# Feed-forward activations in six tiles of their own, at six addresses mod 1024, where one address served all moving tiles

## The chip, the cores and the metric

The kernel runs on one core of a Trainium2 chip. The metric is the device time of one launch in microseconds. Lower is better.

## What is computed

Two layers of a decoder trunk over 256 tokens with 1024 features. Each layer has a feed-forward, four token mixers in parallel, a second feed-forward, and an input embedding under a gate:

```python
def swiglu(u, w_gu, w_down):
    gate, up = jnp.split(u @ w_gu, 2, axis=-1)
    return (jax.nn.silu(gate) * up) @ w_down

for i in range(DEPTH):                                   # DEPTH = 2, D_FF = 2816
    h = h + 0.5 * swiglu(rms_norm(h, ffn1_norm[i]), ffn1_w_gu[i], ffn1_w_down[i])
    h = h + token_mixing(rms_norm(h, mix_norm[i]), ...)  # DeltaNet, mLSTM, S5, MoBA, gates, w_out
    h = h + 0.5 * swiglu(rms_norm(h, ffn2_norm[i]), ffn2_w_gu[i], ffn2_w_down[i])
    h = h + (p[i] @ ple_w_proj[i]) * jax.nn.sigmoid(rms_norm(h, ple_norm[i]) @ ple_w_gate[i])
return rms_norm(h, final_norm)
```

## The kernel before

Features lie on the partitions and the 256 tokens along the free dimension. Every float32 product is made of three matmuls on rounded halves (`mm3`): weights are split into `wh` and `wl`, activations into a high and a low tile, and wh·high, wh·low and wl·high are added in PSUM. Each of the three loads its 128x128 stationary weights anew and streams 256 columns of 4 bytes, so a moving operand is 1024 bytes per partition. In the mixers' transposed projections (`mm3t`) the roles are swapped: there a slice of the activations `xa` is stationary, and the weights `wh`, `wl` move.

Weights arrive by DMA in units of 128x1024 (`raw`). ScalarE rounds a unit to `wh`, and VectorE subtracts to get `wl`. There are four `raw` buffers and six each of `wh` and `wl`.

A feed-forward (`ffn`) runs over 22 tiles f of 128 hidden features. For each f, the gate and up products are 48 matmuls with the moving tiles `xa0`, `xa1` (or, in the second feed-forward of a layer, a tile of the same kind). VectorE and ScalarE then make the activation `act2`: its high half by a copy on ScalarE, its low half by a subtraction on VectorE. With a lag of two tiles (`LAG = 2`), the down product of f - 2 follows: eight output tiles by three matmuls, 24 matmuls with the moving tile `act2`, into four PSUM banks named `acc` (three) and `inv` (one). Down products of the last two tiles come at the end, bank by bank.

`act2` is a tile of the tag `A`, one of four buffers. Tags `A`, `B`, `Y` and `D` lie in the pool `operands` together with `xa0` and `xa1`, behind a pad of `BASE` = 288 bytes. All their sizes are multiples of 1024 bytes, so all of these tiles start at the same address mod 1024, which the title of the change gives as 416. Behind that pool comes the pool of constants, and then the pool of weights behind a pad of `WBASE` bytes; a slice of weights is 512 bytes wide.

The order of the instructions is not the order of the source. A planner (`Plan.order`) runs a list schedule over all instructions with a cost for each, and issues them in the order that it finds. A tile of a tag takes one of the tag's buffers in that schedule, and waits if none is free. The planner's cost of a matmul is the longer of its columns and twice its weights' columns at 2400 per us, and then

```python
(0.007 if views[2].store.tag.startswith("xa") else 0.011)
```

All instructions are issued from one line, 430, which is why tiles and not lines tell them apart in the profile.

## Time and profile before

| what | value |
|---|---|
| time, median of 3 runs | 1336.62 us (1332.21, 1336.62, 1351.59) |
| time of the profiled execution | 1337.75 us |
| its span, from first to last instruction | 1336.0 us |
| TensorE busy share | 98% |
| VectorE, ScalarE busy share | 75%, 55% |
| matmuls | 11366, each with a weight load of its own |

The page's first part gives the busy time of each engine. The second gives the span in 40 slices, with the granted TensorE clock in tenths. Matmuls overlap in the pipeline, so the duration of one matmul (some 0.28 us) is longer than the distance from its start to the start of the next. That distance, here called the pitch, is what the time is made of. It can be read from a table of stretches: the matmuls counted in a stretch are those that overlap it, so the pitch is the width of the stretch plus one duration of 0.28 us, divided by the count.

### The profile page before, as it was taken

How to read it: one execution, taken by the hardware profiler on the slowest of the kernel's cores; microseconds unless marked ns; L12 is line 12 of the kernel's file. 1: busy time of each engine (PE TensorE's matmuls, PEld its weight loads, DVE VectorE, ACT ScalarE, POOL GpSimd, SP SyncE). 2: the span in 40 equal slices, each digit the busy share in tenths (PEclk: the TensorE clock that was granted, in tenths of full speed). 3: DMA queues.
4: the chain of work that ended last, by engine and by line, in shares of the span. 5: the costliest groups of instructions: out<-in, count | busy, mean ns of one | idle time of the engine just before them, and what ended most of it. 6: DMA issues, size and time to landing. Idle time of an engine off the chain costs nothing.

```text
span 1336.0 us, 27989 instructions
## 1 busy us (share of the span) xinstructions
PE 1315.3 (98%) x11366; PEld 1293.7 (97%) x11366; DVE 1003.0 (75%) x1893; ACT 739.7 (55%) x1174; POOL 39.1 (3%) x73
## 2 busy tenths in 40 slices
PE   8999999999999999999999999999989999999997
PEld 7999999988999999999999999999989999999997
DVE  7999557988858866666999965778876778655575
ACT  7655457884445644444655454689635456444453
POOL 2000000000010000000020000000000100000000
PEclk9999999999999999999999999999989999999998
DMA  8665565436636655555566645553466356555651
GB/s 291 182 192 166 187 194 161 147 105 145 204 114 194 189 191 190 191 194 206 166 218 193 190 147 188 173 182 103 136 149 214 110 176 201 197 194 194 203 167 54
DMA packets 81761, 233.67 MB, mean 175 GB/s; under 512 B 20832, under 2 KB 24928, under 8 KB 81632
## 3 DMA queue, kind: packets, MB, share of 16 engines
q1 hardware_dynamic: 81632, 231.88, 55.1%
q8 instruction: 89, 1.46, 0.4%
q14 instruction: 40, 0.33, 0.1%
HBM read 229.49 MB, written 2.36 MB: 174 GB/s over the span
## 4 chain that ended last, share of the span: by engine, by line
PE 88%; DVE 5%; issue 3%; DMA 2%; ACT 1%; SPq 1%; POOL 0%; DVEq 0%; POOLq 0%; ACTq 0%
PE mm L430 63%; PE acc L430 18%; PE inv L430 7%; DVE wl L430 2%; DMA raw<-dm 1%; ACT wh L430 1%; DVE C L430 1%; SPq L430 1%; DMA raw<-in_weights 1%; DVE s5u L430 1%; DMA xc<-in_x 0%; DMA q<-dx 0%; DVE B L430 0%; DVE T L430 0%; DVE A L430 0%
## 5 line engine op out<-in xcount | busy, mean ns | idle before, releaser
L430 PE MATMUL mm<-xa,wh 128*128 128x256 f32 x4288 | 757.6, 279 | 0.7 <-ACT wh L430 0.7
L430 ACT CAST wh<-raw 128x1024 fp32r<-128x1024 f32 (+1 forms) x434 | 437.1, 1038 | 457.4 <-issue 212.9
L430 PEld LDWEIGHTS mm<-xa,wh 128*128 128x128 f32 x4288 | 654.5, 189 | 4.0 <-ACT wh L430 1.2
L430 PE MATMUL mm<-xa,wl 128*128 128x256 f32 x2144 | 598.4, 279 | 0.6 <-DVE wl L430 0.6
L430 DVE TENSOR_TENSOR wl<-raw,wh 128x1024 fp32r<-128x1024 f32 (+1 forms) x434 | 514.1, 1207 | 48.3 <-ACT wh L430 47.5
L430 PEld LDWEIGHTS mm<-xa,wl 128*128 128x128 f32 x2144 | 404.1, 188 | 2.3 <-DVE wl L430 1.3
L430 DVE TENSOR_TENSOR T<-mm,rs 128x512 f32<-128x512 f32 x98 | 67.4, 689 | 171.2 <-PE mm L430 169.6
L430 PE MATMUL acc<-A,wh 128*128 128x256 f32 x1056 | 187.2, 278 | 2.7 <-ACT A L430 2.7
L430 PEld LDWEIGHTS acc<-A,wh 128*128 128x128 f32 x1056 | 160.8, 189 | 3.0 <-ACT A L430 2.9
L430 PE MATMUL acc<-A,wl 128*128 128x256 f32 x528 | 146.2, 278 | 0.0
L430 PE MATMUL mm<-B,wh 128*128 128x256 f32 x576 | 101.0, 278 | 0.0
L430 PEld LDWEIGHTS acc<-A,wl 128*128 128x128 f32 x528 | 99.4, 188 | 0.0
L430 PEld LDWEIGHTS mm<-B,wh 128*128 128x128 f32 x576 | 87.3, 188 | 0.6 <-ACT B L430 0.4
L430 PE MATMUL mm<-B,wl 128*128 128x256 f32 x288 | 79.9, 279 | 0.0
L430 PE MATMUL inv<-A,wh 128*128 128x256 f32 x352 | 65.5, 278 | 0.0
L430 PEld LDWEIGHTS mm<-B,wl 128*128 128x128 f32 x288 | 53.9, 188 | 0.0
L430 PEld LDWEIGHTS inv<-A,wh 128*128 128x128 f32 x352 | 53.8, 189 | 0.0
L430 DVE TENSOR_TENSOR th<-mm,rs 128x512 f32<-128x512 f32 (+1 forms) x41 | 27.6, 676 | 31.4 <-PE mm L430 27.6
L430 PE MATMUL mm<-wh,xa 128*128 128x256 f32 (+1 forms) x256 | 49.3, 285 | 0.0
L430 PE MATMUL inv<-A,wl 128*128 128x256 f32 x176 | 48.8, 277 | 0.0
L430 ACT CAST A<-sg 128x256 fp32r<-128x256 f32 x88 | 35.3, 402 | 14.7 <-DVE sg L430 14.6
L430 PEld LDWEIGHTS mm<-wh,xa 128*128 128x128 f32 x256 | 40.1, 188 | 0.7
(263 smaller groups left out, 1352.8 us busy)
## 6 DMA issues: line engine op xcount, KB each, us to landing
raw<-in_weights SPq DMA_DIRECT2D x420, 512.0 KB, 4.3
raw<-in_weights SPq DMA_DIRECT2D x8, 256.0 KB, 5.1
raw<-in_weights SPq DMA_DIRECT2D x4, 408.0 KB, 3.6
dm<-D SPq DMA_DIRECT2D x4, 256.0 KB, 4.5
raw<-dm SPq DMA_DIRECT2D x16, 64.0 KB, 4.5
out_t<-T SPq DMA_DIRECT2D x4, 256.0 KB, 2.5
xc<-in_x SPq DMA_DIRECT2D x3, 256.0 KB, 4.7
raw<-in_weights SPq DMA_DIRECT2D x2, 272.0 KB, 3.0
```

The source lines that it names most:

```text
L430: getattr(getattr(nc, v.engine), v.name)(*map(real, v.args), **{k: real(x) for k, x in v.kw.items()})
```

## The change

The feed-forwards' `act2` leaves the tag `A`. A new pool `acts` between `operands` and the constants holds six tiles `act0` to `act5`, one buffer each, and hidden tile f takes number f mod 6. Each is 16 columns (64 bytes) longer than its two halves, so that tiles follow each other at steps of 64 bytes mod 1024; the pool begins with a pad of 192 bytes, and `ACTS` gives the columns by which the halves are shifted inside their tile. With 416 as the address of the pool `operands`, the starts are 416 + 192 = 608, then 672, 736 + 64 = 800, 800 + 64 = 864, 864 + 48 = 912 and 928 + 16 = 944 mod 1024. `WBASE` falls from 736 to 160, since the new pool adds 192 + 6 x 2112 = 12864 bytes, which is 576 mod 1024: the weights keep their address mod 1024. All other tiles of the tags `A`, `B`, `Y`, `D` and `xa0`, `xa1` keep theirs.

```diff
-BASE, WBASE = 288, 736
+BASE, WBASE = 288, 160
+ACTS = (0, 0, 16, 16, 12, 4)
...
         self.op.tile([128, BASE // 4], F, tag="pad", name="pad")
+        self.ap = E(tc.tile_pool(name="acts", bufs=1))
+        self.ap.tile([128, 48], F, tag="pad", name="pad")
         self.cp = E(tc.tile_pool(name="const", bufs=1))
...
-            act2 = self.t("A", [128, 2, T], R)
+            at = ACTS[f % len(ACTS)]
+            act2 = nc.tile(self.ap, [128, 2 * T + 16], R, f"act{f % len(ACTS)}", 1)
+            act2 = act2[:, at:at + 2 * T].rearrange("p (a t) -> p a t", a=2)
             ah, al = act2[:, 0], act2[:, 1]
```

## Rows read from the trace of the kernel before

**Rows 1.** The page: engines' busy time, and the granted clock in 40 slices.
```profile
PE 1315.3 (98%) x11366; PEld 1293.7 (97%) x11366; DVE 1003.0 (75%) x1893; ACT 739.7 (55%) x1174; POOL 39.1 (3%) x73
PEclk9999999999999999999999999999989999999998
```

**Rows 2.** Waits of TensorE, whole run: total us, times, longest us.
```profile
PE acc L430 <- DVE D L430: 6.3, 2, 3.5
PE acc L430 <- ACT A L430: 2.7, 1, 2.7
PE mm L430 <- ACT sq L430: 1.6, 1, 1.6
```

**Rows 3.** Groups by form, TensorE, whole run: count | busy us, mean ns | idle before.
```profile
L430 PE MATMUL acc<-A,wh 128*128 128x256 f32 x1056 | 187.2, 278 | 2.7 <-ACT A L430 2.7
L430 PE MATMUL acc<-A,wl 128*128 128x256 f32 x528 | 146.2, 278 | 0.0
...
L430 PE MATMUL inv<-A,wh 128*128 128x256 f32 x352 | 65.5, 278 | 0.0
L430 PE MATMUL inv<-A,wl 128*128 128x256 f32 x176 | 48.8, 277 | 0.0
```

**Rows 4.** Stretches of TensorE: us, busy (matmuls), granted clock, DMA share, GB/s.
```profile
34.00:114.00 80.00, 80.00 (x708) 1.00 0.63 192
127.50:203.50 76.00, 76.00 (x647) 1.00 0.59 187
216.20:220.80 4.60, 4.60 (x39) 1.00 0.80 241
248.50:253.50 5.00, 5.00 (x45) 1.00 0.59 178
324.00:374.00 50.00, 50.00 (x427) 1.00 0.59 186
...
466.30:634.00 167.70, 167.70 (x1482) 1.00 0.59 194
677.40:766.00 88.60, 88.60 (x784) 1.00 0.63 197
775.80:857.80 82.00, 82.00 (x698) 1.00 0.54 174
870.40:875.00 4.60, 4.60 (x38) 1.00 0.76 223
902.60:907.80 5.20, 5.20 (x46) 1.00 0.55 182
983.00:1030.00 47.00, 47.00 (x417) 1.00 0.62 191
...
1122.50:1290.00 167.50, 167.50 (x1480) 1.00 0.59 195
```

**Rows 5.** Two of those stretches again, matmuls with tile A alone.
```profile
127.50:203.50 76.00, 32.08 (x261) 1.00 0.59 187
775.80:857.80 82.00, 32.56 (x264) 1.00 0.54 174
```

**Rows 6.** Order of time, TensorE, 126 to 128 us: start, us, count.
```profile
126.20 0.39 PE L430 MATMUL mm<-xa,wh 128*128 128x256 f32 x2
126.43 1.04 PE L430 MATMUL mm<-cst,C 128*128 128x128 f32 x8
127.22 0.36 PE L430 MATMUL mm<-xa,wl 128*128 128x256 f32 x1
127.42 0.40 PE L430 MATMUL acc<-A,wh 128*128 128x256 f32 x2
```

**Rows 7.** Groups by form in 216.2 to 220.8 us, matmuls of the swapped kind.
```profile
L430 PE MATMUL mm<-wh,xa 128*128 128x272 f32 x26 | 5.0, 289 | 0.0
```

**Rows 8.** Order of time, TensorE, around 230 us: the narrowest frequent moving operand.
```profile
230.00 2.34 PE L430 MATMUL acc<-C,B 128*128 128x64 f32 x20
232.15 0.36 PE L430 MATMUL mm<-xa,wh 128*128 128x256 f32 x1
```

**Rows 9.** Instructions of tile A, 482 to 492 us: ns min/median/max, first start.
```profile
L430 ACT CAST A<-sg x1: 400/400/400, 486.7 to 486.7; 128x256 fp32r<-128x256 f32 x1
L430 DVE TENSOR_TENSOR A<-sg,A x1: 417/417/417, 488.0 to 488.0; 128x256 fp32r<-128x256 f32 x1
```

## The prediction

> **What bounds the kernel now.** I read the page first, then TensorE's waits, its groups by form, and a table of stretches. The page [rows 1] shows TensorE busy 98% of the span, at the full granted clock nearly throughout; VectorE and ScalarE have room. The waits [rows 2] show that TensorE hardly waits: its three longest groups are 6.3, 2.7 and 1.6 us of 1336. So the time is the number of matmuls times the pitch, the distance from one start to the next, and only the pitch, the count or a new wait can move it.

> The pitch is what the table of stretches is for [rows 4]. Take width plus 0.28 us over the count. The stretch 466.3 to 634 gives 167.98 / 1482 = 113.35 ns, and 34 to 114, 677 to 766, 983 to 1030 and 1122 to 1290 give 113.4, 113.4, 113.4 and 113.4. But 127.5 to 203.5 gives 76.28 / 647 = 117.9, 775.8 to 857.8 gives 82.28 / 698 = 117.9, and 324 to 374 gives 117.8. The granted clock is 1.00 in all of them, so this is not the clock. The program is the same kind in both: the first layer's first feed-forward runs its first half at 113.4 and its second half at 117.9, with the same tiles at the same addresses. So one and the same matmul has two steady pitches, 4.5 ns apart (the short and the long one below), and keeps the one that it has. Order of time shows what switches it [rows 6]: at 126.4 us eight small transposes come in between, and behind them the long pitch begins. Within a stretch the pitch outlives the changes from `xa` to `A` and back, since both kinds stand in the stretches counted above. Thus with `xa` and `A` at one address mod 1024 the pitch is something that is handed on.

> **The change part by part.**

> *Counts.* Matmuls with the moving tile `act2` are the groups on `acc` and `inv`: 1056 + 528 + 352 + 176 = 2112 [rows 3], which is 4 feed-forwards x 22 tiles x 24. None is added or removed. The other matmuls of the feed-forwards are 4 x 22 x 48 = 4224, so a feed-forward matmul is an `act2` one in a third of the cases. In the two long-pitched stretches lie 647 + 698 = 1345 feed-forward matmuls [rows 4], 261 + 264 = 525 of them on `A` [rows 5]. I count the other 2112 - 525 = 1587 on `A`, and 4224 - 820 = 3404 on `xa` or its like, as short-pitched.

> *The pool and its buffers.* The planner could change its order if an activation ever waited for a buffer. It does not: f is made while f - 1 and f - 2 wait for their down product, so three are alive, four buffers were enough and six are too. The planner's cost for `act0` is that for `A` (0.011 in both). So I take order, DMAs and weight splits as unchanged, at 0. Were it otherwise, TensorE's wait for `A` is the row to look at, 2.7 us once [rows 2].

> *The two writes.* A ScalarE copy and a VectorE subtraction go to other addresses, 88 of each. What hides them is the lag: the activation made at 486.7 to 488.4 us [rows 9] belongs to the gate and up product that ended near 483, and its down product comes two tiles of 72 x 113.35 ns = 8.2 us later, near 499. Some 11 us of slack cover writes of 0.4 us even if each took twice as long. Without that cover 88 x 0.8 us = 70 us would be exposed, which is not in question here.

> *The pitch of the 2112 matmuls at new addresses.* This is all of the change, and the trace has no matmul with `act2` anywhere but at 416. Bounds come from the nearest rows. From below: twenty matmuls with only 64 moving columns take 232.15 - 230.00 = 2.15 us [rows 8], 107.5 ns each, so with the same 128 columns of weights even a quarter of the moving stream gets no lower. From above: the swapped matmuls move weights, which lie at another address mod 1024 than 416. [...] The same kind with 256 columns gives 5.28 / 45 = 117 and 5.48 / 46 = 119 ns [rows 4].

> These last rows are the nearest in kind: full weights, 256 moving columns, the same three-matmul pattern, another relation of moving to stationary address. They stand at the long pitch, in both layers, while matmuls with the moving operand at 416 are found at either. I therefore take the long pitch, 117.9, for `act2` at the new addresses, and the present mix for everything else.

> [...]

> *The sum.* The profiled execution took 1337.75 us, of which 1336.0 are its span and 1.75 lie around it; that is 1.1 above the median of 1336.62. To it come 1587 x 4.5 ns = 7.1 us; the 525 already there add nothing. 1344.9 us against the profiled execution, 1343.8 against the median: 1344 us.

> **The rivals.**

> *The new addresses bring the short pitch back.* The long pitch is only handed on; a matmul at another address could break it, as the transposes did in the other direction, and six addresses met in turn give six chances every 49 us. Then the 1345 long-pitched feed-forward matmuls turn short: -6.1 us, 1330.6. If the mixers also start better, the 50 us around 350 give another 1.9 us: 1328.7. For it: each of the four feed-forwards has a short-pitched stretch [rows 4], so it is reached again and again after interruptions. Against it: the swapped matmuls.

> *The address does not matter,* or matters so little that the pitch is handed on as before: 1336.6, with stretches falling to either pitch by chance. A stretch of 76 us is worth 647 x 4.5 ns = 2.9 us, and a few such make the distance between the runs of before. [...]

> *The long pitch is handed on to `xa`.* If `act2` leaves TensorE at the long pitch and 416 merely keeps it, all 4991 short-pitched feed-forward matmuls turn long: +22.5 us, 1359. For it: stretches of 76 and 82 us in which nothing turned it back. Against it: only if nearly every one of the six addresses forces it.

> *Slower by over 2%,* the other side. 2% is 26.7 us, about what a measurement of this kernel can tell from no change. With all of `xa` at the long pitch (3404 x 4.5 ns = 15.3 us), 11.4 us are missing, over `A`'s present 1587 x 113.35 + 525 x 117.9 ns = 241.8 us: it decides from an `act2` pitch of 253.2 / 2112 = 119.9 ns. [...] With `xa` as it is, `act2` alone would need (241.8 + 26.7) / 2112 = 127 ns, beyond every row of 256 columns.

> *Faster by over 2%.* `act2` at the lower bound: 2112 x 107.5 = 227.0 us, -14.8; with all other feed-forward matmuls short -3.7 more, and the 50 us of the mixers -1.9: 1316. Even that is 1.5%. So this needs a pitch that the narrowest rows don't show.

> **How the numbers follow.** `act2` at the long pitch, the rest as it is: 0.38. Short pitch brought back: 0.22. Address without effect: 0.17. Long pitch handed on in part or whole, under 2%: 0.12. Slower by over 2%: 0.09. Faster by over 2%: 0.02. The first four make 0.89 for within 2%. The predicted time is that of the likeliest, 1344. The range goes down to the second case with some of the mixers, 1326, and up to the edge of the last but one, 1363; outside lie the two cases beyond 2% and the strays of the second and third. The likeliest case's own range is 1337 to 1352, a stretch or two of chance either way.

> **What would show it.** In the profile after, groups by form should show 2112 matmuls on `act0` to `act5`, with a mean near 281 ns where the pitch is long and 276 where it is short. Steps hold if stretches of `act` tiles stand at 117.9 ns and those of `xa` between them at 113.4. If both stand at 113.4 through whole feed-forwards, the first rival is right; if both at 117.9, the third. Different pitches on different `act` numbers would show an effect of each address. I am wrong on the planner if TensorE waits for an `act` tile or the DMA's stretches move. [...]

## The result and the profile after

The kernel after takes 1347.73 us (median of 20 runs, 1344.76 to 1350.26); the kernel before, run beside it, takes 1336.27 us (20 runs, 1332.21 to 1351.59). The ratio is 1.0056, 95% interval 1.0033 to 1.0078: slower by about 0.6%, inside the 2% that had been called "the same". The medians lie further apart (11.5 us) than the means (8.2 us) or the ratio (7.5 us), because the runs of before are skewed: most lie near 1335, some near 1350. The runs of after lie within 5.5 us of each other.

The profiled execution of after has a span of 1343.8 us against 1336.0, which is 7.8 us more. The page's first part, and TensorE's granted clock in 40 slices, answer to [rows 1]:

```profile
PE 1326.5 (99%) x11366; PEld 1305.1 (97%) x11366; DVE 1003.8 (75%) x1893; ACT 738.9 (55%) x1174; POOL 38.9 (3%) x73
...
PEclk9999999999999999999999999999989999999999
```

Every engine has the same number of instructions, and in the slices the clock looks the same; TensorE alone is busy 11 us longer, some 3 of them in place of idle time. Its longest groups of waits (us in total, times, longest), as in [rows 2]:

```profile
PE acc L431 <- DVE D L431: 6.2, 2, 3.9
PE mm L431 <- ACT sq L431: 1.6, 1, 1.6
PE mm L431 <- POOL halfs L431: 1.0, 1, 1.0
...
PE acc L431 <- ACT act L431: 0.6, 1, 0.6
```

The wait for the activation is 0.6 us where it was 2.7. It comes at 27 us, before the first matmul with `act2`. In the thirteen traces of this document the step that holds it takes 0.8 to 3.0 us: the shortest and the longest are both of kernels with the activations at 416, and the longest is that of before. So this difference is chance. Behind it the granted clock of before fell, which the slices of 33 us hide. The same stretch before and after (us, busy and matmuls, granted clock, DMA share, GB/s):

```profile
30.40:33.70 3.30, 3.30 (x18) 0.50 0.66 194
30.40:33.70 3.30, 3.30 (x31) 1.00 0.80 235
```

At the granted 0.50 the starts stand 213 ns apart (13 steps from 30.82 to 33.60 us), where at 1.00 the short pitch is 113.3. The wait made before some 2.1 us longer. The 18 steps behind it take 3.75 us before and 2.19 after, so the clock made it some 1.6 us longer, and the addresses have next to no part in either. A second fall, near 980 us, stands in both traces at the same length, 6.8 us at 0.50. So nothing was lost to waiting by the change, and the two spans understate what it cost. The groups by form (count | busy us, mean ns of one) show what [rows 3] became:

```profile
L431 PE MATMUL acc<-act,wh 128*128 128x256 f32 x1056 | 192.4, 281 | 0.6 <-ACT act L431 0.6
L431 PE MATMUL acc<-act,wl 128*128 128x256 f32 x528 | 148.1, 281 | 0.0
...
L431 PE MATMUL inv<-act,wh 128*128 128x256 f32 x352 | 67.1, 281 | 0.0
L431 PE MATMUL inv<-act,wl 128*128 128x256 f32 x176 | 49.5, 281 | 0.0
```

The same 2112 matmuls, now 281 ns each instead of 277 or 278. Four stretches inside the four feed-forwards (us, busy and matmuls, granted clock, DMA share, GB/s) stand against [rows 4]; the pitch is again width plus 0.28 us over the count:

```profile
140.00:195.00 55.00, 55.00 (x473) 1.00 0.59 191
500.00:630.00 130.00, 130.00 (x1117) 1.00 0.59 191
790.00:850.00 60.00, 60.00 (x517) 1.00 0.62 199
1150.00:1280.00 130.00, 130.00 (x1118) 1.00 0.58 188
```

That is 116.9, 116.6, 116.6 and 116.5 ns. Before, the first and the third of these places stood at 117.9 and the other two at 113.4 [rows 4]. Now all four feed-forwards are alike, at something in between. Six hidden tiles in a row tell what it is made of. First the six blocks of 24 matmuls with `act`, numbers 0 to 5, in the second feed-forward of layer one (the same view, matmuls with that tile alone):

```profile
472.20:475.70 3.50, 3.01 (x24) 1.00 0.40 136
480.70:484.20 3.50, 2.99 (x24) 1.00 0.25 32
489.10:492.60 3.50, 2.99 (x24) 1.00 0.22 46
497.40:500.90 3.50, 3.01 (x24) 1.00 0.23 34
505.90:509.40 3.50, 3.02 (x24) 1.00 0.15 35
514.20:517.70 3.50, 3.02 (x24) 1.00 0.20 56
```

Busy time is 23 pitches and one duration of 0.28 us: 118.7, 117.8, 117.8, 118.7, 119.1 and 119.1 ns. Then the 48 matmuls with `xa` behind each of them:

```profile
475.00:481.30 6.30, 5.82 (x48) 1.00 0.73 251
483.50:489.70 6.20, 5.82 (x48) 1.00 0.81 250
491.90:498.10 6.20, 5.61 (x48) 1.00 0.79 254
500.20:506.50 6.30, 5.82 (x48) 1.00 0.79 248
508.70:514.80 6.10, 5.61 (x48) 1.00 0.83 253
517.00:523.30 6.30, 5.61 (x48) 1.00 0.73 252
```

With 47 pitches, 5.82 us is 117.9 ns and 5.61 us is 113.4 ns. So every `act` block is at or above the long pitch, and what it leaves behind depends on its number: 0, 1 and 3 leave the long pitch to `xa`, 2, 4 and 5 the short one. The same order comes back every six tiles through all four feed-forwards, but for number 1, below.

From each trace, with a feed-forward counted from the first gate matmul to its last down matmul, the four took 195.1, 180.6, 190.8 and 180.6 us before, and 192.5, 185.4, 191.8 and 185.4 after: +8.0 us together, which is the 7.8 us of the span. By tiles, the steps from one start to the next sum to 242.9 us before and 250.4 after (+7.5) for `act2`, and to 487.9 and 490.0 (+2.1) for `xa` inside the feed-forwards.

These sums hold waits and low-clock steps too. Without the low-clock stretch and steps of 150 ns or more, the mean pitch of `act2` goes from 114.5 to 118.4 ns and that of `xa` from 114.4 to 115.6. Over 2112 and 4224 matmuls that is +8.2 and +5.1 us. Against these 13.3 us stand the 3.7 us that chance cost only before, and 1.4 us in the steps with two waits for DVE's `C` (at 116 and 772 us) that are gone after. Such waits come to 1.2 us before, to 1.7 and 1.8 us in two later kernels whose activations run at the short pitch (all moving tiles at 592, and that kernel 32 on), and to none after, where the activations run slower. So it seems that this slack takes up some of the loss.

### The profile page after: what moved, and what is told of

The parts are those of the page before. It is cut to its first block, busy times and chain, and to the rows that moved or that the text cites. A ratio compares the mean times of both kernels' runs of the same rounds, so it can differ in the third digit from the quotient of the medians.

```text
span 1343.8 us, 27981 instructions
## 1 busy us (share of the span) xinstructions
PE 1326.5 (99%) x11366; PEld 1305.1 (97%) x11366; DVE 1003.8 (75%) x1893; ACT 738.9 (55%) x1174; POOL 38.9 (3%) x73
## 4 chain that ended last, share of the span: by engine, by line
PE 91%; DMA 3%; issue 2%; ACT 2%; DVE 1%; SPq 0%; POOL 0%; DVEq 0%; POOLq 0%; ACTq 0%
PE mm L431 64%; PE acc L431 19%; PE inv L431 7%; DVE wl L431 1%; ACT wh L431 1%; DMA raw<-in_weights 1%; DMA q<-dx 1%; DMA dx<-sg 1%; SPq L431 0%; DMA xc<-in_x 0%; ACT B L431 0%; DMA raw<-dm 0%; DVE th L431 0%; DVE D L431 0%; POOL rcol L431 0%
## 5 line engine op out<-in xcount | busy, mean ns | idle before, releaser
L431 PE MATMUL acc<-act,wh 128*128 128x256 f32 x1056 | 192.4, 281 | 0.6 <-ACT act L431 0.6
L431 PEld LDWEIGHTS acc<-act,wh 128*128 128x128 f32 x1056 | 162.1, 189 | 0.9 <-ACT act L431 0.8
L431 PE MATMUL acc<-act,wl 128*128 128x256 f32 x528 | 148.1, 281 | 0.0
L431 PEld LDWEIGHTS acc<-act,wl 128*128 128x128 f32 x528 | 99.3, 188 | 0.0
L431 PE MATMUL inv<-act,wh 128*128 128x256 f32 x352 | 67.1, 281 | 0.0
L431 PEld LDWEIGHTS inv<-act,wh 128*128 128x128 f32 x352 | 54.5, 189 | 0.0
L431 PE MATMUL inv<-act,wl 128*128 128x256 f32 x176 | 49.5, 281 | 0.0
L431 ACT CAST act<-sg 128x256 fp32r<-128x256 f32 x88 | 35.1, 400 | 10.6 <-DVE sg L431 10.5
```

Source lines behind the costliest of these rows:

```text
L431: getattr(getattr(nc, v.engine), v.name)(*map(real, v.args), **{k: real(x) for k, x in v.kw.items()})
```

## The experiments

Each kernel changes the kernel before. All moving tiles there start at 416 mod 1024 and the weights at 992, unless the diff says otherwise; "16 on" means a start 16 bytes higher.

**Which start gives which pitch.** The first probe puts the 88 activations at 16 starts, 0 to 240 bytes past 416, in steps of 16 and in mixed order, in four buffers 256 bytes apart mod 1024.

```diff
+STARTS = (3, 14, 7, 9, 13, 11, 4, 5, 12, 8, 1, 0, 15, 6, 2, 10, ...)
...
-            act2 = self.t("A", [128, 2, T], R)
+            g, self.nact = self.nact, self.nact + 1
+            at = 4 * STARTS[g]
+            act2 = nc.tile(self.ap, [128, 2 * T + 64], R, f"act{(g + g // 16) % 4}", 1)
+            act2 = act2[:, at:at + 2 * T].rearrange("p (a t) -> p a t", a=2)
```

> The 88 activations of the feed-forwards start at the 16 addresses 0, 16, ..., 240 bytes past 416 (mod 256), in a drawn order, in four tiles that lie 256 bytes apart mod 1024, so that each of the 16 is met five or six times, at different multiples of 256. Theory (the pitch is set by the address mod 256): one number of the 16 gives one pitch and one pitch behind it, whichever tile it is in; 0 past 416 keeps what it meets (113.3 or 117.8 ns), 192 past it (as 608 and 864) gives 118.7 and leaves 117.8, 128 past it (as 800) gives 117.9 and leaves 113.3, 240 and 16 past it (as 912 and 944) give 119.1 to 119.3 and leave 113.3. Rival (the full address mod 1024 counts): the same number gives different pitches in different tiles. Time some 1345 us in both.

One run took 1341.78 us. Blocks with `act`: 176 on, 0 on, 192 on, 80 on.

```profile
481.50:485.00 3.50, 2.96 (x24) 1.00 0.24 63
489.70:493.20 3.50, 2.88 (x24) 1.00 0.17 47
737.80:741.30 3.50, 3.01 (x24) 1.00 0.47 129
1156.50:1160.20 3.70, 2.97 (x24) 1.00 0.19 35
```

And the `xa` blocks behind these four:

```profile
484.00:491.00 7.00, 5.61 (x48) 1.00 0.68 224
492.00:499.00 7.00, 5.60 (x48) 1.00 0.74 221
740.00:748.00 8.00, 5.82 (x48) 1.00 0.66 200
1159.00:1166.00 7.00, 5.82 (x48) 1.00 0.71 227
```

All four were met at the short pitch. The block at 0 stays there ((2.88 - 0.28) / 23 = 113.0, where a hundredth of a microsecond is 0.4 ns). The one at 192 (608 mod 256, as `act0`) runs at 118.7 and leaves 117.9, as `act0` does in the kernel after. Each start gave the same pitch in whichever of the four buffers it fell, and in the kernel after 608 and 864, which are 256 apart, gave 118.7 ns each, as 192 on does here. So at these starts the address counts mod 256. The whole map, from the trace's starts:

| bytes past 416 | pitch when met at the short one, ns | left behind |
|---|---|---|
| 0 | 113.3 | what it met |
| 16, 32, 48, 64 | 119.3, 118.1, 117.0, 119.2 | short |
| 80 | 116.9 | long |
| 96, 112, 128, 144, 160 | 116.8, 118.4, 117.8, 118.3, 119.4 | short |
| 176 | some 11 matmuls of 114 to 130, then 113.3 | short |
| 192 | 118.7 | long |
| 208 | 119.1 | long |
| 224, 240 | 117.3, 119.2 | short |

Met at the long pitch, 192 was seen to leave the short one once; 176 brought it to 113.3 within seven matmuls. The table doesn't hold for every start met at the long pitch: 128, 160, 208 and 224 then left the long one, and 48 did so once in two times. In the kernel after, 800 (128 on) was met at the long pitch each time but once and left the short one every time that `xa` came next. So the address and the pitch met don't settle alone what is left behind. Fifteen of sixteen starts begin dearer than 416, and one of these, 176 on, ends cheap.

**Six tiles without other addresses.** The six tiles of the change, but at 416.

```diff
+        self.ap = E(tc.tile_pool(name="acts", bufs=1))
...
-            act2 = self.t("A", [128, 2, T], R)
+            act2 = nc.tile(self.ap, [128, 2, T], R, f"act{f % 6}", 1)
```

> Six tiles of their own as in the change, but all six at 416 mod 1024, weights at 992 as ever. Theory (address alone): as before, 1336 us, ratio 1.000, with 113.3 and 117.8 ns only. Rival (the six tiles, their buffers or the planner's order cost something): 1340 us or more, ratio above 1.004.

1336.46 us, ratio 1.000 (0.997 to 1.003). The tiles, the buffers and the planner cost nothing; all of the loss is the addresses.

**Is it the moving address, or how it stands to the weights?** Three shifts: weights alone 64 on; everything 64 on; moving tiles 192 and weights 16 on, which is the distance of a tile 176 on.

```diff
-BASE, WBASE = 288, 736
+BASE, WBASE = 288, 800        # weights alone 64 on
+BASE, WBASE = 352, 736        # everything 64 on
```

> The kernel before with the weights 64 bytes further on (32 mod 1024 in place of 992), all moving tiles at 416. Theory (the distance from the stationary to the moving address counts): every matmul with xa, A, B, Y, D now has the distance that 608 and 864 had, 118.7 ns in the feed-forwards: 6850 short-pitched ones by 5.4 ns and 3080 long-pitched ones by 0.9 ns, +40 us, 1376 us. Rival (the moving address alone counts): 1336 us, ratio 1.000.

> The kernel before with moving tiles and weights both 64 bytes further on: moving tiles at 480, weights at 32 mod 1024, the same distance. Theory (distance counts): as before, 1336 us, 113.3 and 117.8 ns. Rival (the moving address alone counts): 480 is a new address, at which the pitch is another; if it is as at most of the six, 118 to 119 ns, +40 us.

Weights alone: 1370.58 us, ratio 1.0246 (1.0203 to 1.0289). Two stretches of all its matmuls, in the first feed-forward and the second:

```profile
140.00:195.00 55.00, 55.00 (x466) 1.00 0.61 197
500.00:630.00 130.00, 130.00 (x1098) 1.00 0.57 183
```

118.6 and 118.7 ns, for `xa` and `A` alike, though neither has moved. It is the pitch of the activations 192 on, and by subtraction the same distance mod 256 (192 forward for the one, 64 back for the other). Moving the weights alone cost 33 us of the 40 that had been worked out.

Everything 64 on: 1339.82 us, ratio 1.0005 (0.998 to 1.003). Its second feed-forwards, one in each layer:

```profile
500.00:630.00 130.00, 130.00 (x1106) 1.00 0.58 187
1150.00:1280.00 130.00, 130.00 (x1149) 1.00 0.59 194
```

117.8 and 113.4: the two pitches of before, and one execution keeps the long one where [rows 4] had the short.

```diff
-BASE, WBASE = 288, 736
+BASE, WBASE = 480, 544
...
-                [nc.tile(self.wp, [128, 1024], R, n, SPLIT_BUFS) for n in ("wh", "wl")])
+                [nc.tile(self.wp, [128, 1088], R, n, SPLIT_BUFS)[:, 4:1028] for n in ("wh", "wl")])
```

> The kernel before with all moving tiles (608 mod 1024) and all stationary weights (240 mod 256) moved so that the distance from stationary to moving address is 112 mod 256 in place of 192, which is what activations 176 bytes past 416 had in the look at 16 starts: there the pitch went to 113.3 ns from either pitch within some five matmuls. Theory (the distance mod 256 decides, and at 112 only the short pitch is steady): nearly all matmuls of 256 columns at 113.3, some 3000 fewer at 117.8, -13 us: 1323 us, ratio 0.990, and the runs lie closer together than the 1332 to 1352 of before. Rival (any distance keeps either pitch for long stretches once all tiles share it): 1336 us, with long stretches at two pitches.

1375.25 us, ratio 1.0286 (1.0263 to 1.0309), a miss: the same two stretches hold

```profile
140.00:195.00 55.00, 55.00 (x460) 1.00 0.61 192
500.00:630.00 130.00, 130.00 (x1101) 1.00 0.58 187
```

which is 120.2 and 118.3 ns, and 113.3 stands nowhere for long. Either long stretches behave otherwise than a block of 24, or the distance is not all. Later experiments take that up.

**Can the long pitch be handed to all of `xa`?** By the map, a tile 80 on leaves the long pitch. All activations there:

```diff
-            act2 = self.t("A", [128, 2, T], R)
+            act2 = nc.tile(self.ap, [128, 2 * T + 64], R, "act", 4)
+            act2 = act2[:, 20:20 + 2 * T].rearrange("p (a t) -> p a t", a=2)
```

> The feed-forwards' activations alone, all at 80 bytes past 416 (mod 256), four buffers. In the look at 16 starts these left the long pitch behind them from either side. Theory (a matmul hands its pitch to the next, and 416 keeps what it is handed): xa and its like at 117.8 throughout the feed-forwards, 3404 by 4.5 ns = 15 us, and the activations near 118.8, 9 us: 1360 us, ratio 1.018. Rival (tiles at 416 find their own pitch, whatever stands before them): 9 us alone, 1345 us, ratio 1.007.

1355.34 us, ratio 1.0149 (1.0117 to 1.0181). The second feed-forward:

```profile
500.00:630.00 130.00, 130.00 (x1103) 1.00 0.58 190
```

118.1 ns over both kinds. The time falls between the theory's 1360 and its rival's 1345, and `xa`, itself left at 416, decides for the theory: its mean pitch in the feed-forwards goes from 114.4 to 117.4 ns (counted as above), which is 12.9 us over 4224 matmuls. In the whole trace the steps of `xa`, waits and low-clock steps included, sum to 779.3 us where before has 768.5 (+10.8), and those of the activations to 250.7 (+7.8). This is the prediction's third rival, made on purpose.

**How fine is it?** The probe again, in steps of one column (4 bytes) around 0 and around 176 on.

```diff
+STARTS = (61, 43, 1, 2, 47, 42, 44, 3, 41, 63, 62, 0, 46, 45, ...)
+            at = STARTS[g]
```

> A second look, in steps of one column: activations at 0, 4, 8, 12, 164 to 188, 244, 248 and 252 bytes past 416. Theory (a distance in bytes mod 256 matters, smoothly or by lines of 16 bytes): neighbours of 176 within a line behave as 176, or the pitch changes by steps between them; no pitch below the 113.3 of 0 and 176, since weight loads of 128 columns alone come no closer than 107.5 to 112 ns. Rival (some start gives less): a block near 109 ns. Time some 1340 us.

One run, 1348.56 us. Blocks 4, 176, 12, 244 and 0 bytes on:

```profile
484.70:488.30 3.60, 3.08 (x24) 1.00 0.27 58
526.50:530.00 3.50, 2.96 (x24) 1.00 0.27 62
509.70:513.20 3.50, 3.02 (x24) 1.00 0.12 35
602.00:605.50 3.50, 3.12 (x24) 1.00 0.21 46
813.30:816.70 3.40, 2.88 (x24) 1.00 0.19 29
```

121.7, 116.5, 119.1, 123.5 and 113.0 ns. By the trace's starts, one column above 416 costs 8 ns a matmul, one below it 5 (118.0), and one column away from 176 on 6 to 9 (119.7 at 172, 122.2 at 180). No start lies below 113.3.

**All moving tiles at the start that ends cheap.** `xa`, `A`, `B`, `Y` and `D` at 592 (176 on), weights at 992. Each moving tile is 256 bytes longer here, so that later tiles start at 592 only mod 256, which is what the first probe found to count.

```diff
-BASE, WBASE = 288, 736
+BASE, WBASE = 448, 64
...
-        self.xa = [nc.tile(self.op, [128, KD, T], R, f"xa{j}") for j in range(2)]
+        self.xa = [self.moved(self.op, [128, KD, T], R, f"xa{j}") for j in range(2)]
...
+        if tag in OPERANDS:
+            return self.moved(self.op, shape, dt, tag, BUFS[tag])
...
+    def moved(self, pool, shape, dt, tag, bufs=None):
+        n = int(np.prod(shape[1:]))
+        x = self.nc.tile(pool, [128, n + 64], dt, tag, bufs)[:, 4:4 + n]
```

> All moving tiles (xa, A, B, Y, D) start at 592 mod 1024, 176 bytes past 416, and the weights stay at 992. In both probes an activation tile 176 bytes past 416 came to 113.3 ns within a block, whichever pitch it met. If that is the only steady pitch there, no long-pitched stretch is left: against the kernel before, whose runs keep 10 to 20 us of long pitch, the time is about 1323 us, ratio 0.990, and the runs lie close together. Rival: as with all tiles 176 on and the weights 16 on, stretches longer than a block find another pitch (118 to 120 ns); then 1337 us or more, up to 1375, ratio 1.00 to 1.03.

1329.40 us (1327.19 to 1331.12), before 1340.44 beside it; ratio 0.9917 (0.9886 to 0.9949), faster than both kernels of the change.

```profile
140.00:195.00 55.00, 55.00 (x487) 1.00 0.60 196
500.00:630.00 130.00, 130.00 (x1149) 1.00 0.60 195
```

113.5 and 113.4 ns: no long-pitched stretch is left, and the seven runs lie within 4 us where those of before spread over 16. Behind an interruption the first 10 or so matmuls still take 114 to 121 ns, and then the pitch is 113.3.

**A few tiles there, to turn the pitch back.** `Y` and every fourth activation at 592, all else at 416.

```diff
-            act2 = self.t("A", [128, 2, T], R)
+            act2 = self.moved(self.ap, [128, 2, T], R, "act", 1) if f % 4 == 3 else self.t("A", [128, 2, T], R)
```

> Every fourth activation tile (f mod 4 = 3) and the mixers' Y tiles start at 592 mod 1024, all else as before (416, weights at 992). If a tile there turns a long pitch short and 416 keeps the short one, each feed-forward is at 113.3 ns from its fourth hidden tile on, at a cost of some 73 ns a block for 22 blocks (1.6 us): the two long-pitched stretches of before give back about 6 us and the mixers some 2 us, which makes 1330 us, ratio 0.995, with runs closer together than before. Rival: the long pitch that is found at the end of a feed-forward or in the mixers comes from what stands there, or 592 leaves the long pitch behind as often as it takes it away: 1337 us, ratio 1.00.

1333.06 us (1331.19 to 1334.53), ratio 0.9948 (0.9923 to 0.9972). All matmuls of layer two's first feed-forward, before and behind its first tile at 592 (the block at 705.9 us):

```profile
680.20:705.80 25.60, 25.60 (x220) 1.00 0.60 191
709.20:733.00 23.80, 23.80 (x212) 1.00 0.61 197
```

117.6 ns until that block, 113.6 behind it, on tiles that stayed at 416. So the short pitch is handed on like the long one, and 24 matmuls are enough to bring it back; the tiles at 592 met the long pitch three times in this trace (705.9, 777.7 and 1151.3 us) and left the short one each time.

**The miss again: joint shifts of 32 and of 16.** The kernel at 592 with everything 32 on (moving tiles 112 mod 256, weights 0), and the kernel before with everything 16 on (moving 176 mod 256, weights 240).

```diff
-BASE, WBASE = 448, 64         # the kernel with all moving tiles at 592
+BASE, WBASE = 480, 64         # the same, everything 32 on
```

```diff
-BASE, WBASE = 288, 736        # the kernel before; moved() as above puts all moving tiles 16 on
+BASE, WBASE = 288, 224
...
+                [nc.tile(self.wp, [128, 1088], R, n, SPLIT_BUFS)[:, 4:1028] for n in ("wh", "wl")])
```

> The kernel with all moving tiles at 592, shifted by 32 bytes as a whole: moving tiles at 112 mod 256 (80 there), weights at 0 mod 256 (224 there). If only the distance of moving and stationary address decides, as in the joint shift by 64, everything settles at 113.3 ns again: about 1329 us, ratio 0.992. Rival: a joint shift matters in itself, as the one by 16 bytes seemed to show; then pitches other than 113.3 stand in the long stretches, 1337 us or more, ratio 1.00 to 1.03.

> The kernel before with moving tiles and weights both 16 bytes on (moving at 176 mod 256, weights at 240). If it was the weights' place 16 bytes off, and not the distance, that gave 118 to 120 ns with everything moved by 176 and 16, then the two pitches of before (113.3 and 117.8) are gone here too: 1350 us or more, ratio over 1.01. Rival: 16 bytes of joint shift are neutral like 64: only 113.3 and 117.8 ns, 1332 to 1345 us, ratio 1.00; then the earlier miss has another cause.

32 on: 1322.50 us (1321.17 to 1325.13), before 1340.57, ratio 0.9881 (0.9831 to 0.9931), the fastest kernel here.

```profile
140.00:195.00 55.00, 55.00 (x487) 1.00 0.61 196
500.00:630.00 130.00, 130.00 (x1148) 1.00 0.60 196
```

16 on: 1327.72 us (1326.10 to 1334.23), ratio 0.9923 (0.9893 to 0.9953).

```profile
140.00:195.00 55.00, 55.00 (x487) 1.00 0.61 196
500.00:630.00 130.00, 130.00 (x1149) 1.00 0.60 195
```

Both stand at 113.5 and 113.4 ns in these stretches. The first came as the distance theory had it: 32 of joint shift, like 64, change no pitch. The second was expected at 1350 or more and is the other way round. The long pitch of before is gone from these stretches, so 16 bytes of joint shift do matter, but the short one is what is left. With the weights on a multiple of 32 bytes, two distances were each tried in whole kernels at two places and behaved alike. With the weights 16 off it, the pitches belonging to those two distances are others: one lost its cheap end, the other its dear one. Long stretches as such are not the cause of the miss, since the kernel at 592 holds 113.3 through whole feed-forwards. What the rule is at 16 off stays open; two points don't make a map. In both kernels with the weights 16 off, the weight tiles are 256 bytes longer as well, and that was not tried alone.

Why 32 on is faster than 592 itself, by 6.9 us between medians, is not the pitch: both hold the same in the feed-forwards. TensorE's longest group of waits, in the mixers,

```profile
PE acc L430 <- DVE D L430: 3.4, 2, 1.7
```

is 3.4 us here and 6.1 us at 592, which is 2.7 of the 5.6 us between their spans. The clock makes up the rest. Behind each of the two waits the granted clock at 592 fell to 0.50, and 32 on, where the longest wait was 1.7 us, it did not. Behind the first wait, at 592 and then 32 on:

```profile
318.60:322.00 3.40, 3.40 (x18) 0.50 0.25 73
315.30:318.70 3.40, 3.40 (x28) 1.00 0.50 163
```

A second such stretch stands at 970.6 us in the trace at 592. With the 213 ns at 0.50 in the trace of before against 113.3 at 1.00, the two stretches of 3.4 us cost some 3.2 us by estimate; with the 2.7 that is 5.9, a little over the 5.6. So this part of the gain of 32 on is no gain in pitch. Why VectorE is earlier there wasn't tried.

## Why the prediction was right, and where only in sum

*The bound.* "Only the pitch, the count or a new wait can move it" held in the main: the counts are the same, no wait was added, and the feed-forwards (+8.0 us) make the change of the span (+7.8). What the prediction put at nothing is chance in the trace that it started from: a longer wait at 27 us and a fall of the clock behind it, 3.7 us together, which the trace of after does not have. The eight transposes that it took for the switch do not set the pitch but let it fall either way: behind those near 775 us the long pitch begins in before, and the short one with six tiles at 416 and with everything 64 on (117.7 ns against 113.3 and 113.3, from 790 to 850 us).

*Counts, pool and writes at 0.* Six tiles at 416 gave a ratio of 1.000, so 0 was right for the buffers and the planner. The ScalarE write takes 400 ns as before, and no wait for it was added, so 0 was right there too.

*`act2` at the long pitch, +7.1 us.* Measured +8.2 by the mean pitch, 114.5 to 118.4 ns (+7.5 with waits and low-clock steps). The size was nearly right. The value taken, 117.9, is what two of the six addresses give when met as they are in the kernel after; the other four give 118.7 to 119.3, so the mean is 118.6. The reason given, the swapped matmuls as the nearest rows, pointed the right way, but no run here isolates them; what the runs show is that nearly every other relation of moving to stationary address starts dearer than 416 (in the first probe fifteen of sixteen starts, fourteen of them at 116.8 to 119.4 ns).

*"The present mix for everything else".* This step failed, and the sum hid it. By its mean pitch `xa` in the feed-forwards came out 5.1 us dearer, against a zero. The mix before is made of long runs of one pitch, handed on for 70 us and more; after, it is dealt out anew at each tile, half and half. In the feed-forwards that stood at the short pitch before, `xa` lost 2.2 us each; in the two that had a long-pitched stretch it stayed within 0.6 us by pitch. (Layer one's first feed-forward won 2.6 us on `xa` in all, by the shorter wait and the clock.) That 1344 came within 4 us of 1347.73 is in part luck: 6 us too little for the pitch against 5 us of waits and clock that fell away.

*The rivals.* Three of them are true of some tiles. "The short pitch brought back" is what 800, 912 and 944 do for the `xa` behind them. "Handed on to `xa`" is what 608 and 864 do, and it was weighed with "only if nearly every one of the six addresses forces it": two of the six force it and a third keeps it, which is half of the blocks of `xa`, so it came in part: 5.1 of the 15.3 us that all of `xa` would cost. With all activations 80 on it gave 1355 us, near the 1359 worked out. "Address without effect" is true of 672 alone, which is 416 + 256: it keeps the pitch it meets. In the first feed-forward it met the short one and stayed at 113.3; elsewhere it met the long one that `act0` had left.

*The bounds.* The upper rows, swapped matmuls of 256 columns at 117 and 119 ns, were of another kind and no true end: the six addresses reached 119.3, and three columns below 416 a block ran at 123, past the 119.9 from which the case of over 2% decides. The lower bound, 107.5, held, but was misread: of the twenty narrow matmuls [rows 8] the first stands 55 ns before the next and the last 84, and the others stand 110 to 112 apart, close under the 113.3 that no start undercut. The other side, slower by over 2%, can be reached, by `xa` and `act2` dear together as the prediction described it, though through the weights: moved alone by 64 bytes, they gave 118.6 on everything and 2.5%.

*The range of before.* That a stretch falling to either pitch makes the distance between runs was right: kernels with one steady pitch spread over 4 us (592, and 32 bytes on from it) and 8 (before, 16 on), the kernel after, which sets the pitch anew every 8 us, over 5.5, and before over 19.

## What to carry to other kernels

When TensorE is the bound and its granted clock stays at 1.00, read the spacing of its matmuls by stretches: if the same code shows two values (here 113.4 and 117.9 ns), look at the start addresses of the moving tile and of the weights mod 256, together and not one by one. Probe the starts with one block each inside a working kernel, and read both what the block costs and what it leaves to its neighbours; then put all moving tiles at one start that ends cheap from either side (here 592, with 113.4 ns in the stretches read), rather than spreading them, and time the whole kernel, since one such choice, with the weights 16 bytes off, came out 2.9% slower. A time that moves between runs by a per cent, as the 1332 to 1352 us of before, can be such a pitch, met by chance and handed on. Before two traces are compared for an effect of a few us, look at the clock in stretches of a few us: a wait and a fall behind it can hide a third of the effect, as here 3.7 of 11.5 us.
